# MLP activations transposed by transfers of their 16-bit halves in place of TensorE with the identity

## The chip, the cores and the metric

The kernel runs on one core of a Trainium2 chip. A core has TensorE (matmuls, called PE in the profile), VectorE (DVE), ScalarE (ACT), GpSimd (POOL) and SyncE (SP), each with its own instruction queue, which is worked off in order, and 16 DMA engines that all queues share. The metric is the device time of one execution in microseconds; the median of several runs counts.

## What is computed

One layer of a diffusion backbone for 128 context tokens and 128 latent tokens, all in float32: a modulation from the conditioning vectors, one combined projection, two attention mixers, a gated merge, and an MLP with a squared ReLU. The part that the change touches:

```python
def sq_relu_mlp(h, w_up, w_down):
    return jnp.square(jax.nn.relu(h @ w_up)) @ w_down

        h2 = rms_norm(xp, norm2_w[l]) * (1 + sc2) + sh2
        xp = xp + g2 * sq_relu_mlp(h2, w_up[l], w_down[l])
```

`D_MODEL` is 2048 and the hidden width `D_FF` is 8192. The same weights serve both groups of tokens, so a weight tile that is loaded once is used for two blocks of 128 tokens.

## The kernel before

Every float32 product is made as three products of a reduced float32 type: the weight tile (`raw`, 128 partitions x 1024, 512 KB) is copied by ScalarE into a high part `wH`, VectorE subtracts to get the low part `wL` (`split`, lines 86 and 234), and TensorE multiplies high by high, high by low and low by high (lines 284 to 286). A weight tile is one step; a plain step is twelve matmuls of 128x512.

All weight tiles stand in one list, `wsteps`. For each step `run()` issues the loads that are due, prepares (splits) the tiles ahead, issues the matmuls, and then calls what is hung on that step with `at(...)`. Two tables by step decide how far ahead this goes: `LOOK` (splits) and `RUN` (loads). For some tiles (`LO_DMA`, `XL_DMA`) the low part is made by ScalarE and an adding transfer of GpSimd instead of VectorE. All tiles of 128x1024 come from one pool of 48 buffers, so a load waits until a buffer is free.

The MLP is the last stage. `w_up` has 16 slices of 512 columns, two to a piece; `w_down` has the matching 16 groups of rows. The order is: up products of piece 0, then for p from 0 to 7 the up products of piece p+1 (`up_pair`) followed by the down products of piece p (`down_unit`, four output slices of four steps, 16 steps). In `up_pair` a position of 256 rows is either plain (two steps, 24 matmuls) or fast: a seven-product scheme after Strassen and Winograd, with 21 matmuls, and with more sums on VectorE and copies on ScalarE. `FAST` lists the fast positions of each piece. At the end of a piece VectorE combines the partial products, and ScalarE applies ReLU and square (`up`, line 1176).

The square of the ReLU then lies with tokens on partitions, and the down product needs the hidden units there. `up_T(n)` does this for slice n: `tT` (line 797 and following) makes eight 128x128 transposes on TensorE against the identity into PSUM, ScalarE copies the high part from PSUM into `aH`, VectorE subtracts for `aL`. `T_PAIR` says, for each piece, at which of the 16 down steps of the piece before this is done; slices 0 and 1 have their own places (two steps after the up product, and inside the first fast position of piece 1). The down products of a piece are used one piece later, so these results are not needed at once.

Sums of the down products over the pieces go to `dsum`: by VectorE, or for the units in `SUM_DMA` by a ScalarE copy and an adding transfer of GpSimd. `AWAY` lists gate tiles of the merge that go to memory and come back `GATE_BACK` steps before they are used, to free buffers.

Of the kernel before, what the change touches and what calls it, by code (L numbers as in the profile page):

```python
# [10 lines left out]
F32 = mybir.dt.float32  # L11
F32R = mybir.dt.float32r
BF16 = mybir.dt.bfloat16
AF = mybir.ActivationFunctionType
OP = mybir.AluOpType
AX = mybir.AxisListType

P = 128
# [10 lines left out]
PIECES = [[2 * i, 2 * i + 1] for i in range(8)]  # L29
# [1 line left out]
LOAD = 4  # L31
FB_DVE = 6
FB1 = 14
H_AT = 41
DOTS1 = [6, 8, 15, 20, 28, 30, 31, 38]
CHUNKS = [2, 2, 2, 4, 6]
NFAST = 8
FAST = {1: (0, 1, 5, 6, 7), 2: (0, 3, 4, 6, 7), 3: (0, 2, 4, 5, 7), 4: (0, 2, 3, 5, 7), 5: (0, 1, 2, 4, 5, 7), 6: (0, 2, 4, 6, 7), 7: (0, 1, 2, 4, 5, 7)}
SUM_DMA = [5, 6, 9, 10, 11, 12, 13, 15, 16, 19, 20, 21, 23, 25, 27]
AWAY = [('gA', 1), ('gB', 0), ('gA', 2)]  # L40
GATE_BACK = 3
DIRECT = (3,)
LO_DMA = [70, 83, 86, 107, 131, 176, 184, 186, 196, 233, 242, 292, 314, 328, 357, 379, 402, 435]
LO_AHEAD = 2

LOOK = "523112344222344433223333332123333453344534332454455544344533333544324554444555556665556644444333333333332222122213444544555434333333342344333334333323445565533344456656533344434444445455564546555554444443322355444554433333333434334433333333333654654332334455554444555653323314333422222223443233333332223323365455454443222212233432443334434743443332222333423323333333333325434322223333433323333334555543365365433333332222554442122132334343222223332233345544"
RUN = "454562331000011222223333322222222222222233345555544455434445554445665555555664543433234334444445665543321222222212444444444444442222222232223344444455544544444444443344343334466644455555554543255444343355556866544443566553333323333345552332222222223445332333333333332211122222332233322211233323323332333223333333332343322211333343333322233333444433643333312222334443322333233322222222322333443434455544333120222222232111233456655566567556322325335553333333"
CONST_AT = [60, 65]
XL_DMA = [40]
ADA_AT = [None, 4, 13, 21, 21, 34, 30]  # L50
XS_AT = {1: 13, 2: 18, 3: 29}
POST = {('kvA', 0): [67, 69, 71], ('qA', 0): [70, 73, 75], ('qA', 1): [74, 76, 82], ('kB', 0): [78, 84, 89], ('qB', 0): [82, 84, 93], ('kB', 1): [85, 90, 93], ('qB', 1): [91, 94, 96]}
JOBS = [[78, 79, 81, 83, 94], [82, 83, 87, 90, 94], [88, 89, 91, 93, 98], [93, 93, 95, 98, 102], [96, 97, 100, 105, 112], [102, 103, 107, 112, 120], [105, 107, 111, 118, 120], [112, 114, 117, 120, 122]]
SS_AT = [48, 56, 66, 75, 139, 139]
T_AT = [4, 4]
PREP_IN = [6, 7]
DOTS = [32, 39, 41, 43, 47, 47, 48, 49, 51, 52, 53, 55, 60, 64, 67, 69, 72, 76, 76, 83, 89, 90, 92, 92, 94, 98, 101, 103, 103, 105, 108, 111, 111, 112, 115, 118, 120, 122, 123, 123, 124, 128, 129, 129, 131, 132, 133, 137, 137, 137, 138, 143, 144, 147, 147, 150, 153, 157, 158, 160, 165, 167, 168, 168, 170, 172, 175, 177, 177, 178, 179, 183]
DOTS2 = [232, 233, 235, 237, 240, 242, 262, 265, 269, 270, 272, 289, 297, 299, 302, 306, 307, 326, 327, 332, 334, 335, 358, 361, 364, 365, 368, 370, 393, 394, 397, 401]
STAT_AT = [-1, -1, 10, 12]
# [5 lines left out]
def tile_hybrid_step(ctx: ExitStack, tc: tile.TileContext, a):  # L65
# [10 lines left out]
    def G(name, dt=F32):  # L76
        return gp.tile([P, 1024], dt, name=name, tag="g")
# [7 lines left out]
    def copy(out, in_):  # L85
        act.activation(out, in_, AF.Copy)  # L86
# [99 lines left out]
    wsteps = []  # L186
    cal = {}

    def at(i, fn):
        cal.setdefault(i, []).append(fn)  # L190
# [361 lines left out]
    def end_of(key):  # L552
        return max(st["i"] for st in wsteps if st["key"] == key)
# [238 lines left out]
    def tT(src, hi, lo):  # L792

        for s in range(2):
            ps = bank("ps_T")
            for k in range(4):
                pe.transpose(ps[:, k * P:(k + 1) * P], src[:, s, k * P:(k + 1) * P], ident)  # L797
            psv = ps.rearrange("p (k t) -> p k t", k=4)
            copy(hi[:, :, s, :], psv)
            dve.tensor_tensor(lo[:, :, s, :], psv, hi[:, :, s, :].bitcast(F32), op=OP.subtract)  # L800

    def HL(name):
        return [G(name + x, F32R).rearrange("p (k s t) -> p k s t", k=4, s=2) for x in "HL"]
# [254 lines left out]
    def up_pair(p):  # L1058
# [32 lines left out]
        for pos, is_fast in enumerate(kinds):  # L1091
# [50 lines left out]
            def mm_y(st, b=b, j=j, pos=pos, end=end):  # L1142
                u0, u1 = (G(f"up{n}").rearrange("p (s n) -> p s n", s=2) for n in (n0, n1)) if end else (None, None)
                if end:
                    copy(u0[:, 0, :], box["Q1"])
                lo, hi = slice(0, 512), slice(512, 1024)
                todo = [("Q6", sc(j, 1), b["uH"][:, lo], b["uL"][:, lo]), ("Q2", x(j, 1, 0), b["YB"][:, lo], b["YB"][:, hi]),
                        ("Q7", sc(j, 2), b["tH"][:, hi], b["tL"][:, hi]), ("Q4", x(j, 1, 1), b["uH"][:, hi], b["uL"][:, hi]),
                        ("Q5", sc(j, 0), b["tH"][:, lo], b["tL"][:, lo])]
                if end or pos == 0:  # L1150
                    todo.append(("Q3", sc(j, 3), b["XH"][:, hi], b["XL"][:, hi]))
                if not end:
                    todo = [todo[i] for i in ((1, 2, 0, 4, 5, 3) if pos == 0 else (1, 4, 2, 3, 0))]
# [13 lines left out]
                for name, stat, h, l in todo:  # L1167
                    mm(name, stat, h, l, end)
                    for out, i0, i1, op in post.get(name, []):
                        dve.tensor_tensor(out, *(box[v] if isinstance(v, str) else v for v in (i0, i1)), op=op)  # L1170
                b.clear()
                if end:
                    for n, u in ((n0, u0), (n1, u1)):
                        up_r[n] = u
                        for f in (AF.Relu, AF.Square):
                            act.activation(u.rearrange("p s n -> p (s n)"), u.rearrange("p s n -> p (s n)"), f)  # L1176
                    box.clear()
# [271 lines left out]
```

## Time and profile before

| | us |
|---|---|
| runs | 1347.2, 1346.38, 1343.57 |
| median | 1346.38 |
| the profiled execution | 1346.98 |
| its span, first to last instruction | 1344.9 |

The profile is of one execution. Busy times are given by engine and by stretch of time; a busy TensorE is not TensorE at its peak, because matmuls overlap and each row shows a matmul's whole passage, so its pace is read from the starts of matmuls that follow each other. The MLP's weight steps run from about 675 us to the end; the transposes of line 797 for the MLP lie between 681 and 1288 us, sixteen groups of eight. In this kernel ScalarE issues one transfer of its own, at the start; all weight loads are issued by SP. In a row of the groups stand line, engine, operation, names, shapes and count, then busy us and mean ns, then the idle time before, with what ended it. In a timeline row stand start, length, engine, line, operation, names, count, and in brackets the idle time before it.

### The profile page before, as it was taken

What the parts mean: (1) busy time and instruction counts of PE and PEld (TensorE: products, weight loads), DVE (VectorE), ACT (ScalarE), POOL (GpSimd) and SP (SyncE); (2) the same over time, 40 slices, a digit from 0 to 9 for tenths busy, and PEclk for the clock granted to TensorE, in tenths of its full rate; (3) what the DMA queues carried; (4) which work ended last, traced back from release to release, by engine and by line L of the source; (5) the groups of instructions that cost most, each with busy time, mean ns of one, the idle gap of its engine ahead of it and who ended that gap; (6) DMA issues with size and microseconds to landing.
All of it is one profiled execution on the core that took longest, in us unless ns stands there. A gap on an engine that the chain in (4) does not pass through costs nothing.

```text
span 1344.9 us, 18331 instructions
## 1 busy us (share of the span) xinstructions
PE 1331.6 (99%) x6552; PEld 1081.6 (80%) x6552; DVE 1194.9 (89%) x1568; ACT 738.8 (55%) x966; POOL 66.7 (5%) x76
## 2 busy tenths in 40 slices
PE   8899999999999999999999999999999999999998
PEld 4577788888788878888888888888888888888887
DVE  4689999988898999998789999998999999899675
ACT  5524443566656544345666665565665656556540
POOL 0000001332000000000000000000000000000000
PEclk9899999999999999999999999999999999999999
DMA  9999998977688999798466666888798887769942
GB/s 370 410 409 408 404 366 352 375 215 271 193 282 299 377 397 344 284 332 290 175 232 230 240 219 245 271 264 279 231 317 239 265 285 216 267 191 302 373 151 93
DMA packets 109611, 385.44 MB, mean 287 GB/s; under 512 B 12368, under 2 KB 13584, under 8 KB 109520
## 3 DMA queue, kind: packets, MB, share of 16 engines
q1 hardware_dynamic: 104064, 365.05, 73.5%
q0 software_dynamic: 5312, 19.14, 7.5%
q8 instruction: 51, 0.84, 0.3%
q14 instruction: 40, 0.33, 0.1%
q10 hardware_dynamic: 144, 0.08, 0.0%
HBM read 369.25 MB, written 7.11 MB: 280 GB/s over the span
## 4 chain that ended last, share of the span: by engine, by line
PE 96%; DMA 3%; DVE 1%; issue 0%; ACT 0%; SPq 0%; DVEq 0%
PE acc L284 17%; PE acc L286 17%; PE acc L285 17%; PE Q L1068 6%; PE Q L1070 6%; PE Q L1069 6%; PE acc L384 4%; PE acc L386 4%; PE acc L385 4%; PE ps_ada L301 2%; DMA raw<-in_w_in 2%; PE ps_T L797 1%; PE ps_S L700 1%; DMA araw<-in_w_pair 1%; PE Z L1070 1%; PE Z L1069 1%
## 5 line engine op out<-in xcount | busy, mean ns | idle before, releaser
L234 DVE TENSOR_TENSOR wL<-raw,wH 128x1024 fp32r<-128x1024 f32 x361 | 430.7, 1225 | 79.6 <-ACT wH L86 72.6
L86 ACT ACTIVATE wH<-raw 128x1024 fp32r<-128x1024 f32 (+1 forms) x385 | 385.6, 1047 | 138.6 <-PE acc L285 33.0
L384 PE MATMUL acc<-wH,hH 128*128 128x512 f32 x276 | 109.9, 398 | 0.0
L386 PE MATMUL acc<-wH,hL 128*128 128x512 f32 x276 | 108.4, 393 | 0.7 <-DVE hL L90 0.7
L385 PE MATMUL acc<-wL,hH 128*128 128x512 f32 x276 | 108.5, 393 | 0.0
L284 PE MATMUL acc<-wH,hH 128*128 128x512 f32 x256 | 101.8, 398 | 0.0
L286 PE MATMUL acc<-wH,hL 128*128 128x512 f32 x256 | 99.8, 390 | 0.0
L285 PE MATMUL acc<-wL,hH 128*128 128x512 f32 x256 | 99.7, 389 | 0.0
L1278 DVE CUSTOM_DVE_ANT_0 aT<-aT,cB,cols 128x1024 f32<-128x1024 f32 x56 | 71.5, 1284 | 0.2
L1278 DVE CUSTOM_DVE_ANT_0 junk<-aT,cB,cols 128x1024 bf16<-128x1024 f32 x56 | 71.3, 1279 | 0.0
L86 ACT ACTIVATE tH<-t 128x1024 fp32r<-128x1024 f32 x37 | 39.3, 1062 | 56.9 <-DVE t L1123 42.0
L384 PEld LDWEIGHTS acc<-wH,hH 128*128 128x128 f32 x276 | 52.3, 190 | 14.2 <-issue 3.3
L386 PEld LDWEIGHTS acc<-wH,hL 128*128 128x128 f32 x276 | 52.4, 190 | 12.3 <-DVE hL L90 1.1
L385 PEld LDWEIGHTS acc<-wL,hH 128*128 128x128 f32 x276 | 52.4, 190 | 10.5
L86 ACT ACTIVATE uH<-raw 128x1024 fp32r<-128x1024 f32 x37 | 39.3, 1063 | 36.2 <-DVE raw L1128 35.2
L286 PEld LDWEIGHTS acc<-wH,hL 128*128 128x128 f32 x256 | 48.1, 188 | 10.3
L285 PEld LDWEIGHTS acc<-wL,hH 128*128 128x128 f32 x256 | 48.1, 188 | 9.6 <-issue 0.2
L284 PEld LDWEIGHTS acc<-wH,hH 128*128 128x128 f32 x256 | 48.1, 188 | 9.6 <-issue 0.2
L1123 DVE TENSOR_TENSOR t<-raw 128x1024 f32<-128x1024 f32 x37 | 45.1, 1220 | 5.8 <-PE Z L1069 1.9
L1176 ACT ACTIVATE up<-up 128x1024 f32<-128x1024 f32 x28 | 29.7, 1062 | 33.0 <-DVE up L1170 32.6
L86 ACT ACTIVATE dsum<-acc 128x512 f32<-128x512 f32 x38 | 22.0, 595 | 45.2 <-PE acc L286 42.1
L1133 DVE TENSOR_TENSOR uL<-raw,uH 128x1024 fp32r<-128x1024 f32 x37 | 45.1, 1219 | 0.1
(629 smaller groups left out, 3320.4 us busy)
## 6 DMA issues: line engine op xcount, KB each, us to landing
raw<-in_w_in SPq DMA_DIRECT2D x133, 512.0 KB, 6.7
raw<-in_w_down SPq DMA_DIRECT2D x128, 512.0 KB, 5.9
araw<-in_w_pair SPq DMA_DIRECT2D x80, 512.0 KB, 9.6
raw<-in_w_upF SPq DMA_DIRECT2D x74, 512.0 KB, 5.2
aT<-in_w_gT SPq DMA_DIRECT2D x64, 512.0 KB, 6.6
raw<-in_w_up SPq DMA_DIRECT2D x54, 512.0 KB, 5.1
aT<-in_w_adaT SPq DMA_DIRECT2D x48, 512.0 KB, 7.4
raw<-in_w_out SPq DMA_DIRECT2D x32, 512.0 KB, 9.5
```

The costliest lines, as they stand in the source:

```text
L86: act.activation(out, in_, AF.Copy)
L234: dve.tensor_tensor(st["lo"], st["raw"], st["hi"].bitcast(F32), op=OP.subtract)
L284: pe.matmul(acc[tb], sh, wh[:, k, :], start=f, stop=False)
L285: pe.matmul(acc[tb], sh, wl[:, k, :], start=False, stop=False)
L286: pe.matmul(acc[tb], sl, wh[:, k, :], start=False, stop=l)
L384: pe.matmul(acc[tb], sh, wh[:, k, :], start=kt == 0 and k == 0, stop=False)
L385: pe.matmul(acc[tb], sh, wl[:, k, :], start=False, stop=False)
L386: pe.matmul(acc[tb], sl, wh[:, k, :], start=False, stop=last and k == 1)
L1068: pe.matmul(acc, stat[0], hi, start=f, stop=False)
L1069: pe.matmul(acc, stat[0], lo, start=False, stop=False)
L1070: pe.matmul(acc, stat[1], hi, start=False, stop=l)
L1278: dve.tensor_tensor_reduce(out, box["raw"], cB[s, tag], 1.0, dst if second else baT[:, part, fb:fb + 1], OP.mult, OP.add, dst)
```

## The change

`up_T` no longer uses TensorE. It is cut in two. `up_planes(n)` splits each 32-bit word of the activation into its two 16-bit halves: two ScalarE copies from a strided 16-bit view of the tile into two planes of 128x1024, and after each a transposing transfer of that plane, 256 KB from SBUF to SBUF, issued from ScalarE's queue. Some steps later `up_T(n)` puts the transposed halves together again with four ScalarE copies of 128x512 16-bit values into a float32 tile, and splits that tile as a whole (one copy, one subtraction of 128x1024). `P_PAIR` and `P_UP` place the first part, `T_PAIR` and `T_UP` the second. Per slice two transfers, six 16-bit copies and one 128x1024 split stand in place of eight transposes, two 128x512 copies and two 128x512 subtractions from PSUM.

Most tables are also set anew: fast positions fall from 37 to 35 (pieces 1 and 4 have four), `SUM_DMA` from 15 units to 14, `LO_DMA` from 18 tiles to 17, `XL_DMA` rises from one to two, two more gate tiles go to memory and back, and some digits of `LOOK` and `RUN` and some places in the early stages move by a step or a few.

```diff
-H_AT = 41
+H_AT = 37
-FAST = {1: (0, 1, 5, 6, 7), 2: (0, 3, 4, 6, 7), 3: (0, 2, 4, 5, 7), 4: (0, 2, 3, 5, 7), 5: (0, 1, 2, 4, 5, 7), 6: (0, 2, 4, 6, 7), 7: (0, 1, 2, 4, 5, 7)}
-AWAY = [('gA', 1), ('gB', 0), ('gA', 2)]
-GATE_BACK = 3
+FAST = {1: (0, 1, 5, 7), 2: (0, 2, 3, 6, 7), 3: (0, 2, 4, 5, 7), 4: (0, 2, 5, 7), 5: (0, 1, 2, 3, 5, 7), 6: (0, 2, 4, 6, 7), 7: (0, 1, 2, 4, 6, 7)}
+AWAY = [('gA', 1), ('gB', 0), ('gA', 2), ('gA', 0), ('gB', 2)]
+GATE_BACK = 4
...
-T_PAIR = [[11, 11], [7, 15], [13, 13], [16, 16], [9, 9], [12, 12], [12, 12]]
+T_PAIR = [[5, 9], [8, 12], [8, 10], [9, 11], [8, 11], [10, 11], [8, 11]]
+P_PAIR = [[1, 4], [4, 6], [4, 5], [5, 6], [4, 6], [6, 6], [4, 6]]
+P_UP = [2, 2]
+T_UP = [6, 7]
...
+    def halves(name):
+        return gp.tile([P, 2048], U16, name=name, tag="g")
+
+    planes = {}
+
+    def up_planes(n):
+        src = up_r.pop(n).rearrange("p s n -> p (s n)").bitcast(U16).rearrange("p (c h) -> p h c", h=2)
+        pl, planes[n] = halves(f"pl{n}"), halves(f"plT{n}")
+        for h in range(2):
+            copy(pl[:, 1024 * h:1024 * h + 1024], src[:, h, :])
+            act.dma_start_transpose(planes[n][:, 1024 * h:1024 * h + 1024].rearrange("p (j t) -> p j t", t=P),
+                                    pl[:, 1024 * h:1024 * h + 1024])
+
     def up_T(n):
         aH[n], aL[n] = HL(f"a{n}")
-        tT(up_r.pop(n), aH[n], aL[n])
+        full = G(f"aF{n}")
+        dst = full.bitcast(U16).rearrange("p (k s t h) -> p h s k t", k=4, s=2, h=2)
+        pT = planes.pop(n).rearrange("p (h s k t) -> p h s k t", h=2, s=2, k=4)
+        for h in range(2):
+            for st in range(2):
+                copy(dst[:, h, st], pT[:, h, st])
+        split(aH[n].rearrange("p k s t -> p (k s t)"), aL[n].rearrange("p k s t -> p (k s t)"), full)
...
-        if n != PIECES[0][1]:
-            at(end_of(("up", n)) + 2, lambda: up_T(n))
+        at(end_of(("up", n)) + P_UP[n], lambda: up_planes(n))
+        at(end_of(("up", n)) + T_UP[n], lambda: up_T(n))
...
-                    if p == 1:
-                        up_T(PIECES[0][1])
...
-            for n, i in zip(PIECES[p + 1], T_PAIR[p]):
-                at(len(wsteps) + i, lambda n=n: up_T(n))
+            for n, i, j in zip(PIECES[p + 1], P_PAIR[p], T_PAIR[p]):
+                at(len(wsteps) + i, lambda n=n: up_planes(n))
+                at(len(wsteps) + j, lambda n=n: up_T(n))
```

More of the change, by code (lines that the diff above doesn't have):

```diff
@@ L13 @@
 BF16 = mybir.dt.bfloat16
+U16 = mybir.dt.uint16
 AF = mybir.ActivationFunctionType
@@ L37 @@
 NFAST = 8
-FAST = {1: (0, 1, 5, 6, 7), 2: (0, 3, 4, 6, 7), 3: (0, 2, 4, 5, 7), 4: (0, 2, 3, 5, 7), 5: (0, 1, 2, 4, 5, 7), 6: (0, 2, 4, 6, 7), 7: (0, 1, 2, 4, 5, 7)}
-SUM_DMA = [5, 6, 9, 10, 11, 12, 13, 15, 16, 19, 20, 21, 23, 25, 27]
-AWAY = [('gA', 1), ('gB', 0), ('gA', 2)]
-GATE_BACK = 3
+FAST = {1: (0, 1, 5, 7), 2: (0, 2, 3, 6, 7), 3: (0, 2, 4, 5, 7), 4: (0, 2, 5, 7), 5: (0, 1, 2, 3, 5, 7), 6: (0, 2, 4, 6, 7), 7: (0, 1, 2, 4, 6, 7)}
+SUM_DMA = [5, 6, 9, 10, 11, 12, 15, 19, 20, 21, 23, 25, 26, 27]
@@ L42 @@
+AWAY = [('gA', 1), ('gB', 0), ('gA', 2), ('gA', 0), ('gB', 2)]
+GATE_BACK = 4
 DIRECT = (3,)
-LO_DMA = [70, 83, 86, 107, 131, 176, 184, 186, 196, 233, 242, 292, 314, 328, 357, 379, 402, 435]
+LO_DMA = [70, 83, 86, 107, 131, 176, 184, 196, 233, 242, 292, 314, 328, 357, 379, 402, 435]
 LO_AHEAD = 2
-LOOK = "523112344222344433223333332123333453344534332454455544344533333544324554444555556665556644444333333333332222122213444544555434333333342344333334333323445565533344456656533344434444445455564546555554444443322355444554433333333434334433333333333654654332334455554444555653323314333422222223443233333332223323365455454443222212233432443334434743443332222333423323333333333325434322223333433323333334555543365365433333332222554442122132334343222223332233345544"
@@ L50 @@
[L50 to L54, printed above, removed]
-T_AT = [4, 4]
@@ L59 @@
-STAT_AT = [-1, -1, 10, 12]
-T_PAIR = [[11, 11], [7, 15], [13, 13], [16, 16], [9, 9], [12, 12], [12, 12]]
+LOOK = "423112345333444433223333332123333453344534332454455544344533333544324554444555556665556644444333333333332222122213444544555434333333342344333334333323445565533345456656533344434444445455564547666654444443322355444554433333333434334433333333333654654332334455443444555653323314332311122223443233333332223323365455454443222212233432443334434743443332222333423323333333333325434322223333433323333334555543365365433233332222554442122132334343222223332233345544"
@@ new lines @@
+RUN = "454562220000011222223333322222222222222233345555555455434445554445665555555664543433234334444445665543321222222212444444444444442222222232223344444455544544444444443344333334466644455555554543255444343355556866555554566553333323333345552332222233334556443443333333332211122222332233322211233323323332333223333333332343322211333343333322233333444433643332212222334443322333233322222222322333443434455544333120222222232111233456655566567556322325335553333333"
+CONST_AT = [59, 65]
+XL_DMA = [40, 45]
@@ new lines @@
+ADA_AT = [None, 4, 13, 21, 21, 35, 30]
+XS_AT = {1: 11, 2: 18, 3: 30}
+POST = {('kvA', 0): [67, 69, 71], ('qA', 0): [70, 73, 75], ('qA', 1): [74, 76, 82], ('kB', 0): [79, 83, 88], ('qB', 0): [82, 84, 92], ('kB', 1): [84, 89, 92], ('qB', 1): [91, 94, 96]}
+JOBS = [[78, 79, 81, 83, 94], [82, 83, 87, 90, 94], [88, 89, 91, 93, 98], [93, 93, 95, 98, 102], [96, 97, 100, 105, 112], [102, 103, 107, 112, 120], [105, 107, 111, 118, 120], [112, 114, 118, 121, 123]]
+SS_AT = [49, 56, 66, 75, 139, 139]
+T_AT = [4, 4]
@@ new lines @@
+PREP_IN = [4, 7]
+DOTS = [32, 39, 40, 42, 47, 47, 48, 49, 51, 52, 53, 55, 60, 64, 67, 69, 72, 76, 76, 83, 89, 90, 92, 93, 94, 98, 101, 103, 103, 105, 108, 111, 111, 112, 115, 118, 120, 122, 123, 123, 124, 128, 129, 129, 131, 132, 133, 137, 137, 137, 138, 143, 144, 147, 147, 150, 153, 157, 158, 159, 164, 166, 167, 167, 169, 171, 176, 176, 177, 178, 182, 187]
+DOTS2 = [232, 233, 235, 237, 240, 242, 262, 265, 269, 270, 272, 289, 297, 299, 302, 306, 307, 326, 327, 332, 334, 335, 358, 361, 364, 365, 368, 370, 393, 395, 397, 401]
@@ L61 @@
+STAT_AT = [-1, -2, 10, 11]
+T_PAIR = [[5, 9], [8, 12], [8, 10], [9, 11], [8, 11], [10, 11], [8, 11]]
+P_PAIR = [[1, 4], [4, 6], [4, 5], [5, 6], [4, 6], [6, 6], [4, 6]]
+P_UP = [2, 2]
+T_UP = [6, 7]
 COL = {"qA": 0, "kvA": 1024, "qB": 1536, "kB": 2560, "vB": 3584, "gA": 4608, "gB": 6656}
```

6 lines of the change are left out of this document (removed).

## The prediction

> **What bounds the kernel now.** I read the page first, then the sums by stretch, then single rows of the MLP stage.
>
> ```profile
> span 1344.9 us, 18331 instructions
> PE 1331.6 (99%) x6552; PEld 1081.6 (80%) x6552; DVE 1194.9 (89%) x1568; ACT 738.8 (55%) x966; POOL 66.7 (5%) x76
> PE 96%; DMA 3%; DVE 1%; issue 0%; ACT 0%; SPq 0%; DVEq 0%
> ```
>
> The chain that ended last is 96% TensorE. A busy TensorE need not be at its peak, so the stretches come next (busy time and count for each engine, granted clock, DMA share and rate).
>
> ```profile
> core 0: us, PE busy (x) PEld busy (x) DVE busy (x) ACT busy (x) POOL busy (x), PEclk, DMA share, GB/s
> 0.00:60.00 60.00, 51.47 (x308) 29.14 (x308) 28.73 (x53) 33.40 (x56) 2.00 (x10) 0.94 1.00 388
> 500.00:675.00 175.00, 175.00 (x806) 145.64 (x805) 158.24 (x222) 90.71 (x123) 5.05 (x8) 1.00 0.81 288
> 675.00:1345.00 670.00, 665.17 (x3000) 551.76 (x2998) 601.80 (x700) 393.09 (x449) 21.63 (x25) 1.00 0.74 245
> ```
>
> The MLP stage is the last 670 us. VectorE is busy for 90% of it, ScalarE for 59%, the DMA engines for 74%. Whether TensorE waits there is read from starts: first the 1st and the 9th weight step of the down products of piece 0, eight steps of twelve matmuls apart; then the transposes of two slices between two matmuls.
>
> ```profile
> 739.67 0.39 PE L284 MATMUL acc<-wH,a0H 128*128 128x512 f32 x1
> ...
> 761.43 0.39 PE L284 MATMUL acc<-wH,a0H 128*128 128x512 f32 x1
> ...
> 1286.34 0.39 PE L286 MATMUL acc<-wH,a12L 128*128 128x512 f32 x1
> 1286.57 1.91 PE L797 MATMUL ps_T<-ident,up 128*128 128x128 f32 x16
> 1288.24 0.48 PE L284 MATMUL acc<-wH,a12H 128*128 128x512 f32 x1
> 1288.55 0.40 PE L285 MATMUL acc<-wL,a12H 128*128 128x512 f32 x1
> ```
>
> (761.43 - 739.67) / 96 = 0.227 us from matmul to matmul, 2.72 us a step. 3000 instructions in 670 us, of which 128 are transposes, are (670 - 5 of tail - 128 x 0.11) / 2872 = 0.227 us each: TensorE runs at this pace through the whole stage, with no gap. So only TensorE work that goes away shortens it, and any new lateness of a weight tile lengthens it.
>
> **The change part by part.** *Removed from TensorE:* all transposes of MLP activations.
>
> ```profile
> L797 PE MATMUL ps_T<-ident,up x128: 270/272/273, 681.4 to 1288.2; 128*128 128x128 f32 x128
> ```
>
> A row says 272 ns, but they overlap. From L286 at 1286.34 to L285 at 1288.55 are 2.21 us; two matmul paces are 0.45, so sixteen transposes cost 1.76, 0.110 each: 128 x 0.110 = 14.0 us, all on the path. *Added to TensorE:* FAST lists 35 positions instead of 37 (one fewer in pieces 1 and 4). A fast position is 21 matmuls, two plain steps are 24: 6 x 0.227 = 1.4 us. Net -12.7 us.
>
> *ScalarE* gets the work. Rows of its groups in the MLP stretch (busy us, mean ns | idle before):
>
> ```profile
> L86 ACT ACTIVATE wH<-raw 128x1024 fp32r<-128x1024 f32 x172 | 172.2, 1052 | 38.1 <-PE acc L285 8.5 <-DMA raw<-in_w_down 8.5 <-PE acc L286 5.6
> L86 ACT ACTIVATE uH<-raw 128x1024 fp32r<-128x1024 f32 x37 | 39.3, 1063 | 36.2 <-DVE raw L1128 35.2 <-PE acc L285 1.0
> L86 ACT ACTIVATE YB<-raw 128x512 fp32r<-128x512 f32 x37 | 23.0, 621 | 10.1 <-DMA raw<-in_w_upF 5.0 <-PE Q L1069 2.1 <-issue 1.5
> L86 ACT ACTIVATE dsum<-acc 128x512 f32<-128x512 f32 x38 | 22.0, 595 | 45.2 <-PE acc L286 42.1 <-PE acc L285 2.1
> L86 ACT ACTIVATE a3H<-ps_T 128x512 fp32r<-128x512 f32 x2 | 1.1, 628 | 0.0
> ```
>
> Per slice, two plane copies of 128x1024 (by the uH row 1.06 each; the 16-bit form is not in the trace), four copies of 128x512 that put the halves together (0.55 to 0.62 by the a3H and YB rows), and one split of 1.06 come in place of two copies at 0.55: 2.1 + 2.4 + 1.06 - 1.1 = 4.4, times 16 is 71 us. Two fast positions fewer take back 2 x (3 x 1.06 + 0.62) - 4 x 1.05 = 3.4, two sums fewer by POOL 1.2. 393 + 66 = 459 of 657 us, 70%: no bound on the mean, but it comes in bursts, and ScalarE's wH copies feed every matmul.
>
> *The transfers.* 32 are added, 256 KB each, issued from ScalarE's own queue: while it issues one, the next wH waits behind it. The trace has no transposing transfer. Nearest rows: the one transfer that ScalarE issues, a common load on SP, and how those land.
>
> ```profile
> L94 ACTq DMA_DIRECT2D cols<-in_cols x1: 407/407/407, 0.7 to 0.7; - x1
> L208 SPq DMA_DIRECT2D raw<-in_w_upF x74: 327/328/1722, 651.5 to 1226.0; - x74
> DMA to landing us min/median/max: 3.3/6.1/14.7
> ```
>
> Lower bound 0.33 us; upper bound eight such issues, 2.6 us, if each 128x128 square of the 128x1024 source is pushed by itself. I take the ScalarE row, 0.41, the same engine and the same kind of request. Call it X. In piece 1 all four transfers stand one behind the other, so this is where to try it:
>
> ```profile
> 825.07 0.39 PE L284 MATMUL acc<-wH,a2H 128*128 128x512 f32 x1
> ...
> 830.56 2.15 ACT L1176 ACTIVATE up<-up 128x1024 f32<-128x1024 f32 x2 [0.36 <-DVE up L1170]
> 832.62 5.79 ACT L86 ACTIVATE wH<-raw 128x1024 fp32r<-128x1024 f32 x6
> 846.39 1.28 ACT L86 ACTIVATE dsum<-acc 128x512 f32<-128x512 f32 x2 [7.98 <-PE acc L286]
> ```
>
> Down step 0 starts at 825.07 (my zero). The six wH end at 838.41, at 13.3 (0.95 apart: 2.15 for two dependent squares is 1.09 apart, so waiting for an own result costs about 0.1). Then four times (1.06 + 0.1 + X) = 4.6 + 4X; the two evacuations 1.28, possible once TensorE has done step 7 at 21.8; wH of step 10, 0.95; its split on VectorE with the handover, 1.3. Step 10 is due at 27.2. 13.3 + 4.6 + 1.3 + 0.95 + 1.3 + 4X = 21.5 + 4X: in time up to X = 1.4, and beyond that 4 us of stall per us. Today the cover is the idle 7.98 us in the last row. The same sum for the other pieces (they begin 5.4 to 6.8 us after their step 0) has its limit at X = 1.1 (piece 2), 1.5 (3), 2.0 (4), 1.9 (5), 1.45 (6).
>
> Piece 0 is the tight one, its planes come at steps 1 and 4. Its squares end 6.75 us after step 0 (746.42 against 739.67). Up to the wH of step 8 ScalarE has five wH (4.75), four planes with their issues (4.64 + 4X), two evacuations (1.28), one wL copy (1.06), the wH of step 8 itself (0.95): 19.4 + 4X, with the split 20.7 + 4X. At 0.41 that is 22.4 against 21.8, 0.6 late; then the joining and split of slice 2 (2.3 + 1.06) and wH of step 9 make another 1.6. I book 2.2 us for piece 0 and nothing for the rest; at X = 2.6 the same sums give 10.9, 4.7, 6.0, 4.3, 2.3, 2.9 and 4.6, together 35.7. The first two slices, transposed within the up products of piece 1, I book at nothing: the wH there run ahead behind the same kind of idle time.
>
> The joining copies wait for the landing, and with them every later wH and, behind a split that waits for ScalarE, VectorE's queue. In piece 1 the first joining comes about 9 us after its issue, against 6.1 us median landing today.
>
> [...]
>
> *DMA engines, SP, POOL.*
>
> ```profile
> q1 hardware_dynamic: 104064, 365.05, 73.5%
> q0 software_dynamic: 5312, 19.14, 7.5%
> SPq L208 <- PE Q L1070: 137.6, 60, 7.8
> SPq L208 <- PE acc L286: 131.8, 37, 9.3
> ```
>
> q1 uses 0.735 x 1345 / 365 = 2.7 us of all engines per MB, q0 5.3. 32 x 0.26 = 8.4 MB more are 23 to 44 us, in 26% x 670 = 174 us of free time: nothing on the path. A weight load now may have to wait until a transposing transfer that took the same completion counter eight transfers earlier has landed; SP mostly waits for TensorE to free a buffer (the last two rows, its longest waits in the MLP stretch), which covers it. Two more gates that go to memory and back (2.1 MB, 6 us at q1's price) fall where the DMA share is 0.81 and TensorE has no gap: nothing. POOL adds one sum less and one other load more: nothing.
>
> *VectorE.*
>
> ```profile
> L234 DVE TENSOR_TENSOR wL<-raw,wH 128x1024 fp32r<-128x1024 f32 x164 | 194.3, 1220 | 36.7 <-ACT wH L86 34.0 <-issue 2.6
> L1126 DVE TENSOR_TENSOR raw<-t,raw 128x512 f32<-128x512 f32 x37 | 25.6, 692 | 1.3
> 683.65 1.28 DVE L800 TENSOR_TENSOR a0L<-ps_T,a0H 128x512 fp32r<-128x512 f32 x2
> ```
>
> One split of 1.22 per slice for two of 0.64: -1 us. A fast position is four subtractions or sums of 1.22 and three of 0.69, 6.95, against 2.44 for two plain splits: two fewer are -9. Two more sums into dsum: +1.4. About 593 of 657 us: its share stays at 90%, no gain and no loss.
>
> *Start.* Tables of the first stages move by a few steps. TensorE is idle for 8.5 of the first 60 us while the DMA share is 1.00; I allow 2 us either way and take 0.
>
> Sum: profiled execution 1346.98 us (span 1344.9 and 2.1 around it) - 14.0 + 1.4 + 2.2 = 1336.5. The median of the runs, 1346.38, lies 0.6 below that execution, so 1336.
>
> The PSUM banks of the transposes come free, which nothing on the path waits for today; the transposes of slice 1, which stood inside the first fast position, leave it.
>
> **The rivals.** *1, slower: the issue blocks ScalarE.* If X is near 2.6, wH of the steps 8 to 12 come late in each piece: 1346.98 - 12.7 + 35.7 = 1370. It decides from X = 1.7, where the same sums give 12.5 us and the gain is gone. For it: SP's longest issue took 1.72 us, and a destination of 128x8x128 is cut finer than any transfer here. Against it: 512 KB loads cost 0.33 whatever their destination tile.
>
> *2, slower: the transfers land late.* If each takes its queue for 9.6 us, as the longest wait of this kind now, the second half of a slice lands 19 us after the first issue, the joining waits some 10 us, of which 3 are covered: 7 x 16 = 112 us, 1446.
>
> ```profile
> SPq L208 <- DMA dsum<-dsum: 22.8, 4, 9.6
> ```
>
> It decides from a landing of about 12 us. For it: the engines are 74% busy with loads queued ahead. Against it: the median of 6.1 us for twice the bytes. [...]
>
> *3, no change:* X between 1.5 and 1.85, or the start's tables and a late VectorE eating 9 to 13 us: 1342 to 1350.
>
> *4, it does not save what is removed:* if transposes hid in gaps, nothing would come back. The pace of 0.227 on both sides of them excludes all but a trace of it; it is counted in 3.
>
> **How the numbers follow.** Forecast 0.48, rival 1 0.33, rival 2 0.10, rival 3 0.09. 0.3% (4 us) is about what a measurement of this kernel can tell from no change. Faster 0.48, same 0.09, slower 0.43. The forecast's own range is 1332 (TensorE work alone, 1333.7, less 2 for the start) to 1341 (X = 1.4). For 8 in 10 the top must reach into rival 1: 1368 leaves out its last part and rival 2.
>
> **What would show it.** TensorE should show only the 32 transposes of the merge under the helper's line, and still 0.227 us from matmul to matmul between 500 us and the end. The issue on ScalarE's queue shows X: at 0.4 the forecast holds, above 1.7 rival 1. A wait of VectorE's wL for ScalarE's wH well over 34 us, or gaps of TensorE before down steps 8 to 12, show ScalarE late; a wait of the joining copies on the transfers shows rival 2. ScalarE's busy time should be near 805 us, VectorE's near 1186. Wrong prices of the 16-bit copies (over 1.4 us) would move the limits of X below 1 and make it wrong too.

## The result, and the profile after

The changed kernel takes 1409.97 us (median of 4 runs, 1407.19 to 1418.45) against 1346.22 for the kernel before beside it: a ratio of 1.0487, 95% interval 1.044 to 1.0535. Forecast were 1336 and a range of 1332 to 1368. The profiled execution is 1410.92, its span 1409.1. Up to 675 us the two traces agree within a microsecond or two; all of the loss lies in the MLP stage.

From the page of the changed kernel: the span, the busy times, the chain that ended last by engine, and the group of VectorE's splits.

```profile
span 1409.1 us, 18206 instructions
...
PE 1343.6 (95%) x6429; PEld 1079.3 (77%) x6430; DVE 1187.3 (84%) x1544; ACT 804.5 (57%) x1040; POOL 65.1 (5%) x75
...
PE 72%; DMA 7%; ACT 7%; DVE 6%; ACTq 4%; issue 3%; DVEq 0%; SPq 0%
...
L238 DVE TENSOR_TENSOR wL<-raw,wH 128x1024 fp32r<-128x1024 f32 x366 | 436.9, 1225 | 134.3 <-ACT wH L90 133.2
```

The chain was 96% TensorE and is 72% now; ACT and ACTq (ScalarE's own issuing) have entered it, DMA's share has risen from 3% to 7% and VectorE's from 1% to 6%. The busy times of ScalarE (804.5) and VectorE (1187.3) are those forecast (805, 1186): the work was counted rightly, and what was wrong is when it is done. Now the MLP stretch, in the columns used before.

```profile
675.00:1410.00 735.00, 678.49 (x2883) 550.45 (x2881) 594.41 (x675) 460.65 (x525) 21.57 (x25) 0.96 0.78 236
```

2883 instructions in 735 us; before, 3000 stood in 670 without a gap. At the old pace the work left is 665 - 14.0 + 1.4 = 652.4, plus 5 of tail; the stage lasts 734, so 77 us were lost. Taking from each start-to-start distance the usual pace of its kind accounts for 75 of them: about 59 us of gaps, and about 16 us by which TensorE's matmuls were slower at half clock. Both are seen at the worst place, the down products of piece 6. First ScalarE's queue there (a timeline: start, length, what, idle before), then TensorE's.

```profile
1310.64 7.10 ACTq L1004 DMA_TRANSPOSE plT<-pl  x1
1317.79 2.95 ACT L90 ACTIVATE wH<-raw 128x1024 fp32r<-128x1024 f32 x3 [8.64 <-issue]
...
1326.60 11.87 ACTq L1004 DMA_TRANSPOSE plT<-pl  x1
1338.57 1.08 ACT L90 ACTIVATE dsum<-acc 128x512 f32<-128x512 f32 x2 [12.00 <-issue]
1339.54 1.06 ACT L90 ACTIVATE wH<-raw 128x1024 fp32r<-128x1024 f32 x1
```

```profile
1329.34 0.39 PE L290 MATMUL acc<-wH,a12L 128*128 128x512 f32 x1
1340.65 0.80 PE L288 MATMUL acc<-wH,a13H 128*128 128x512 f32 x1 [10.92 <-ACT wH L90]
1341.91 0.80 PE L289 MATMUL acc<-wL,a13H 128*128 128x512 f32 x1 [0.47 <-DVE wL L238]
1342.50 0.63 PE L290 MATMUL acc<-wH,a13L 128*128 128x512 f32 x1
1342.93 0.63 PE L288 MATMUL acc<-wH,a13H 128*128 128x512 f32 x1
```

ScalarE reaches a transposing transfer at 1326.60 and is let go at 1338.5. Two evacuations and the next `wH` have stood behind it in the queue; the `wH` ends at 1340.6, and in that moment TensorE, idle for 10.92 us, goes on. Before some issues ScalarE's queue stands too: in the trace the issues of 1306.80 and 1310.64 follow an idle 0.74 and 1.49 us, and each comes 0.08 us after the landing (1306.72 and 1310.56) of the transfer that last used the same one (103 and 108) of the eight completion counters, 100, 101, 103 to 105 and 108 to 110 in the trace, which SP's loads and ScalarE's transfers take in turn (in the trace of before all 725 transfers of the two queues do). Then its matmuls are 0.43 apart (1342.50 to 1342.93), not 0.227: the granted clock is halved, as a window inside it shows (PEclk is the third number from the end):

```profile
1341.50:1344.00 2.50, 2.09 (x5) 1.71 (x6) 0.35 (x1) 2.47 (x4) 0.00 (x0) 0.50 1.21 174
```

The half clock appears in nine stretches of the stage ahead of its tail, 3.4 to 13.7 us long, 55 us together, each beginning in or behind a gap; before the change there was none. Every stretch is one to four times 3.41 us long. The length of a wait alone does not tell whether one follows: at 760 us two waits of 0.91 and 0.76 us, one matmul apart, were followed by a slow stretch, and one wait of 2.68 us that began at 1235.9 was not.

The transfers themselves, by their line, and ScalarE's two new kinds of copies:

```profile
L1004 ACTq DMA_TRANSPOSE plT<-pl x32: 1248/1255/11867, 683.7 to 1326.6; - x32
...
DMA to landing us min/median/max: 3.1/5.7/20.0
```

```profile
L90 ACT ACTIVATE aF<-plT 128x512 uint16<-128x512 uint16 x64 | 42.4, 766 | 0.0
...
L90 ACT ACTIVATE pl<-up 128x1024 uint16<-128x1024 uint16 x32 | 33.7, 1052 | 33.9 <-issue 28.1 <-PE acc L290 5.8
```

X, the issue time, is 1.25 us at the least and at the median, three times the 0.41 taken, and 11.87 at the worst. Over all 32 rows it adds up to 64.4 us, 24 of them beyond 1.25 each. What waits for it, in the sums of waits in the MLP stage (us, times, longest), of ScalarE, VectorE, TensorE and SP:

```profile
ACT wH L90 <- issue: 30.9, 10, 8.6
...
ACT pl L90 <- issue: 28.1, 17, 2.8
ACT dsum L90 <- issue: 13.7, 2, 12.0
```

```profile
DVE wL L238 <- ACT wH L90: 91.2, 27, 16.6
```

```profile
PE acc L288 <- ACT wH L90: 19.0, 7, 10.9
PE Q L1094 <- ACT dsum L90: 9.4, 3, 6.2
```

```profile
SPq L212 <- DMA plT<-pl: 35.0, 8, 10.4
```

ScalarE's copies wait behind issues, VectorE's splits wait for ScalarE (34.0 us before, 91.2 now), and TensorE for both; `dsum` is an evacuation of the PSUM banks that the next up product (`Q`) needs. The last row is something else: eight weight loads on SP were held until a transposing transfer had landed. The longest of these waits ends at 1325.55, 0.08 us after the transfer of 1306.80, which had used the load's completion counter (103), landed.

At the same place the load rate falls. Three windows, the last number being GB/s:

```profile
1298.00:1306.00 8.00, 8.00 (x37) 6.60 (x37) 4.40 (x6) 7.57 (x8) 0.00 (x0) 1.00 1.03 373
1306.00:1326.00 20.00, 17.37 (x70) 13.74 (x69) 6.09 (x6) 7.51 (x9) 0.86 (x1) 0.91 1.15 233
1326.00:1345.00 19.00, 7.61 (x25) 5.52 (x24) 2.00 (x2) 6.97 (x10) 0.85 (x1) 0.69 1.16 207
```

The DMA engines are full in all three (their share, the number before it, is 1.03 to 1.16), but move 373 GB/s before the first transposing transfer of this piece and 207 to 233 beside them.

So four things can hold the loss: the hold of ScalarE's queue (theory A), a wait of the joining copies for landings (B), transfers that slow or hold the weight loads (C), and the added copies with the new tables. The experiments take them apart.

### The profile page after: what moved, and what is told of

Read it like the earlier page. It is cut to its first block, busy times and chain, and to the rows that moved or that the text cites. A ratio compares the mean times of both kernels' runs of the same rounds, so it can differ in the third digit from the quotient of the medians.

```text
span 1409.1 us, 18206 instructions
## 1 busy us (share of the span) xinstructions
PE 1343.6 (95%) x6429; PEld 1079.3 (77%) x6430; DVE 1187.3 (84%) x1544; ACT 804.5 (57%) x1040; POOL 65.1 (5%) x75
## 4 chain that ended last, share of the span: by engine, by line
PE 72%; DMA 7%; ACT 7%; DVE 6%; ACTq 4%; issue 3%; DVEq 0%; SPq 0%
PE acc L289 11%; PE acc L290 11%; PE acc L288 11%; PE Q L1094 5%; PE Q L1095 5%; PE Q L1096 5%; PE acc L388 4%; PE acc L390 4%; PE acc L389 4%; ACTq L1004 4%; PE ps_ada L305 2%; DMA raw<-in_w_in 2%; DVE wL L238 2%; ACT wH L90 2%; ACT pl L90 2%
## 5 line engine op out<-in xcount | busy, mean ns | idle before, releaser
L238 DVE TENSOR_TENSOR wL<-raw,wH 128x1024 fp32r<-128x1024 f32 x366 | 436.9, 1225 | 134.3 <-ACT wH L90 133.2
L90 ACT ACTIVATE pl<-up 128x1024 uint16<-128x1024 uint16 x32 | 33.7, 1052 | 33.9 <-issue 28.1
L1094 PE MATMUL Q<-tH,sH 128*128 128x512 f32 x70 | 29.6, 423 | 15.5 <-ACT dsum L90 9.4
```

The lines of the kernel that those rows point to most:

```text
L238: dve.tensor_tensor(st["lo"], st["raw"], st["hi"].bitcast(F32), op=OP.subtract)
L1094: pe.matmul(acc, stat[0], hi, start=f, stop=False)
```

## The experiments

All times are medians, the ratio with its 95% interval is to the kernel before on the same chip (1345 to 1346 us in every set). "Hold" is the time that ScalarE's queue is held for the issues, added over their rows, or by what stands in their place, from its start to the start of the next copy. For issues a hand-over comes on top: around the 64 us of rows of the changed kernel ScalarE idles for 72 us.

| kernel | us | ratio | hold on ScalarE, us |
|---|---|---|---|
| before without MLP transposes | 1338.69 | 0.9933 to 0.9971 | none |
| before with the new tables | 1357.35 | 1.0067 to 1.0112 | none |
| changed, no transfers | 1351.33 | 1.0025 to 1.0061 | none |
| changed, plain transfers | 1358.25 | 1.0074 to 1.0119 | 15 |
| changed, transfers from SP | 1358.73 | 1.0081 to 1.0121 | none |
| changed, short fillers | 1363.28 | 1.0115 to 1.0155 | 36 |
| changed, long fillers | 1398.41 | 1.038 to 1.0423 | 72 |
| changed, fewer loads ahead | 1406.95 | 1.0404 to 1.0521 | 60 |
| changed, transfers unread | 1409.44 | 1.0448 to 1.0492 | 66 |
| **changed** | 1409.97 | 1.044 to 1.0535 | 64 |
| changed, old tables | 1415.09 | 1.0493 to 1.0555 | 71 |
| changed, whole transfers | 1417.90 | 1.0466 to 1.0563 | 83 |
| changed, halved transfers | 1430.52 | 1.0606 to 1.0691 | 89 |

**What the removed transposes were worth.** The kernel before, without the eight transposes of a slice: the split reads the square of the ReLU as it lies.

```diff
-        tT(up_r.pop(n), aH[n], aL[n])
+        src = up_r.pop(n)
+        for s in range(2):
+            v = src[:, s, :].rearrange("p (k t) -> p k t", k=4)
+            copy(aH[n][:, :, s, :], v)
+            dve.tensor_tensor(aL[n][:, :, s, :], v, aH[n][:, :, s, :].bitcast(F32), op=OP.subtract)
```

> The kernel of before without the 128 transposes of the MLP: each slice is split where it lies (same copies and subtractions, read from SBUF in place of PSUM); the transposition itself is left out. If TensorE's work is what sets the MLP stage, 128 x 0.110 = 14 us go: 1332 us. If another engine would set it as soon as TensorE has less to do, 1340 to 1346.

1338.7: 7.3 us come back, half of the 14.0. TensorE has gaps it did not have; its largest waits in the MLP are

```profile
PE Q L1072 <- ACT dsum L86: 1.9, 2, 1.1
PE Q L1073 <- DVE XL L1135: 1.1, 2, 0.7
```

so with TensorE quicker the others begin to be late, in many small gaps. No version of this change can be expected below 1338.7, as long as the rest stays.

**The tables.** The new tables with TensorE's transposes, and the changed kernel with the tables of before (only the four tables that place the new parts stay):

```diff
 (before)
-T_PAIR = [[11, 11], [7, 15], [13, 13], [16, 16], [9, 9], [12, 12], [12, 12]]
+T_PAIR = [[5, 9], [8, 12], [8, 10], [9, 11], [8, 11], [10, 11], [8, 11]]
...
 (changed)
-FAST = {1: (0, 1, 5, 7), 2: (0, 2, 3, 6, 7), 3: (0, 2, 4, 5, 7), 4: (0, 2, 5, 7), 5: (0, 1, 2, 3, 5, 7), 6: (0, 2, 4, 6, 7), 7: (0, 1, 2, 4, 6, 7)}
+FAST = {1: (0, 1, 5, 6, 7), 2: (0, 3, 4, 6, 7), 3: (0, 2, 4, 5, 7), 4: (0, 2, 3, 5, 7), 5: (0, 1, 2, 4, 5, 7), 6: (0, 2, 4, 6, 7), 7: (0, 1, 2, 4, 5, 7)}
...
```

> All new tables of the change, with the transposes still on TensorE (at the new steps of T_PAIR; slice 1 where it was). If the tables alone are harmless: 1346.4 + 1.4 for two fast positions fewer = 1348 us, at most 1352. If the loss comes from the tables (fewer loads ahead, gates away, other steps): 1380 to 1410.

> The changed kernel with every table of before that has a counterpart (FAST, AWAY, GATE_BACK, LOOK, RUN, the start's tables); only P_PAIR, T_PAIR, P_UP and T_UP stay new. If the new tables hold a part of the loss (with TensorE's transposes they cost 11 us): 1395 to 1402. If they only follow the transfers: 1410 to 1425.

1357.35 and 1415.09. Beside TensorE's transposes the new tables cost 11 us, more than the 1348 to 1352 of harmless tables and far from the 1380 to 1410 that would make them the loss. Beside the transfers they may gain 5, which the scatter of the two kernels (1413 to 1419 and 1407 to 1418) leaves open; most of the loss is not in them. Which of the tables costs the 11 us was not tried.

**The copies alone, and plain transfers.** The changed kernel without its transfers (the joining copies read the planes as they are), and with plain transfers of the same bytes at the same places.

```diff
-            act.dma_start_transpose(planes[n][:, 1024 * h:1024 * h + 1024].rearrange("p (j t) -> p j t", t=P),
-                                    pl[:, 1024 * h:1024 * h + 1024])
+            act.dma_start(planes[n][:, 1024 * h:1024 * h + 1024], pl[:, 1024 * h:1024 * h + 1024])
```

> The changed kernel without its 32 transposing transfers: all ScalarE copies stay, and the joining copies read the planes directly; the transposition is left out. If the loss comes from issuing or landing the transfers: 1334 to 1342 us. If ScalarE's 112 added copies are enough to make it late: 1385 to 1410.

> The changed kernel with plain transfers of the same 256 KB from plane to plane in place of the transposing ones; the transposition is left out. If the long issue of a transposing transfer (1.25 us and more, against 0.33 to 0.41 for a plain one) or its own slowness in the DMA engines makes the loss: 1334 to 1345 us. If any 256 KB transfer between SBUF tiles, queued among the weight loads, lands too late: 1370 to 1410.

1351.3 and 1358.3, both between the ranges expected. Even transfers that cost nothing would leave this kernel 5 us behind the one before: against 1338.7 the copies and tables cost 12.6. How this divides between copies and tables is not shown; the tables alone cost 11 beside TensorE's transposes. In the kernel without transfers TensorE waits longest for an evacuation that stands behind ScalarE's other work:

```profile
PE Q L1092 <- ACT dsum L90: 7.3, 3, 4.4
```

The plain transfers tell that their number and bytes are worth 7 us. They issue in 0.47 us, close to the 0.41 of the forecast, and land in 5.0 us at the median against 5.7, though in 8.7 and not 20.0 at worst; being transposing costs another 52 us.

```profile
L1004 ACTq DMA_DIRECT2D plT<-pl x32: 472/472/520, 682.5 to 1284.6; - x32
...
DMA to landing us min/median/max: 2.3/5.0/8.7
```

In the DMA engines the two are not alike either. The rows of ScalarE's queue (packets, MB, share of the time of 16 engines), of the changed kernel and of this one:

```profile
q10 hardware_dynamic: 33936, 8.48, 4.4%
```

```profile
q10 hardware_dynamic: 4752, 8.47, 1.7%
```

For the same bytes that is 0.044 x 1409 = 62 us of all engines against 0.017 x 1357 = 23.

**Who pays: the reader, the queue, or the loads.** Two edits of the changed kernel. In the first the transfers are issued as ever, but the joining copies read the planes that ScalarE wrote; in the second SP issues them.

```diff
 (unread)
-        pl, planes[n] = halves(f"pl{n}"), halves(f"plT{n}")
+        pl, plT = halves(f"pl{n}"), halves(f"plT{n}")
+        planes[n] = pl
...
 (from SP)
-            act.dma_start_transpose(planes[n][:, 1024 * h:1024 * h + 1024].rearrange("p (j t) -> p j t", t=P),
+            sync.dma_start_transpose(planes[n][:, 1024 * h:1024 * h + 1024].rearrange("p (j t) -> p j t", t=P),
```

> The changed kernel, but the joining copies read the planes as ScalarE wrote them and not what the transfers wrote: the 32 transposing transfers are issued at the same places and go through the same buffers, but no joining copy waits for a landing (the transposition is left out). Theory A (the issue holds ScalarE's queue, 40 us of regular issue plus the blocked ones): about as slow as the changed kernel, 1395 to 1415. Theory B (the joining copies wait for late landings): near the kernel with plain transfers, 1355 to 1365. Theory C (the transposing packets slow the weight loads beside them, whoever issues or reads them): 1395 to 1415 like A; the next two runs tell A from C.

> The changed kernel with the 32 transposing transfers issued from SP's queue and not from ScalarE's; all else stays. Theory A (the issue holds ScalarE): ScalarE loses the hold, 1355 to 1370. Theory C (the transposing packets slow the weight loads): 1395 to 1415, or more, since SP's load issues now stand behind the blocked ones.

1409.4 and 1358.7. The joining copies' waiting for a landing costs nothing (theory B falls; SP's loads still wait 35.6 us for landings in that kernel); taking the issue off ScalarE brings back 51 us. SP's rows of that kernel:

```profile
L1004 SPq DMA_TRANSPOSE plT<-pl x32: 1237/1288/7397, 683.7 to 1282.7; - x32
...
DMA to landing us min/median/max: 3.1/4.3/18.0
```

The issue takes SP as long as it took ScalarE (1.29 us at the median against 1.25), blocked ones of up to 7.40 us too, 62 us in all; but SP mostly waits anyway (543 of the stage's 682 us, by the rows of its waits), and the kernel ends with plain transfers' time. Issue times and landings (3.1 to 18.0 us, and 3.1 to 20.0 from ScalarE) are much the same from either queue; the loss comes with the queue that the issues stand in.

**The hold rebuilt without transfers.** In place of each transfer, ScalarE copies 16-bit values for about as long, into the buffer that the transfer would fill: once the same short copy at each place, once by a list of the 32 recorded issue times.

```diff
-            act.dma_start_transpose(planes[n][:, 1024 * h:1024 * h + 1024].rearrange("p (j t) -> p j t", t=P),
-                                    pl[:, 1024 * h:1024 * h + 1024])
+            copy(fill[:, 0:1216], flat[:, 0:1216])
...
+    hold = [1.33, 1.25, 1.25, 1.25, 1.25, 3.75, 1.25, 1.25, 1.25, 2.28, 1.25, 1.63, 1.26, 1.61, 1.48, 2.42,
+            2.01, 1.25, 1.25, 1.46, 1.25, 1.25, 1.25, 1.26, 1.31, 1.91, 1.25, 1.25, 1.25, 7.10, 1.71, 11.87]
...
+            left = hold.pop(0) + 0.17
+            parts = -(-int(left * 1000) // 1800)
+            w = int((left / parts - 0.1) / 0.000833)
+            for _ in range(parts):
+                copy(fill[:, 0:w], flat[:, 0:w])
```

> The changed kernel with each transposing transfer replaced by a ScalarE copy of about the same hold (128x1216 of 16 bits, 1.25 us by the median issue) into the buffer that the transfer would fill; no transfer is left, the joining copies read the planes as they are (the transposition is left out). Theory A in its regular part (32 x 1.25 us of ScalarE): 1375 to 1390, against 1351 without transfers. If only the blocked issues, the landings or the loads beside them matter: 1352 to 1362.

> The changed kernel without transfers, with ScalarE held at each of the 32 places by copies for as long as the issue there took in the trace of the changed kernel (1.25 us at most places, 3.75, 7.10 and 11.87 at the worst; 64 us in all, and the 0.17 us of hand-over around each). No DMA packet is added; the joining copies read the planes as they are (the transposition is left out). Theory A in full (the hold of ScalarE's queue, regular and blocked, is the whole loss): 1395 to 1412. Theory D (half of it: the rest are weight loads that run beside the transposing packets or wait on SP until a transfer has landed): 1375 to 1390.

The short fillers gave 1363.3. From a filler's start to that of the next copy are 1.11 us (two rows of its timeline), 35.5 us for 32:

```profile
749.17 1.20 ACT L90 ACTIVATE plT<-up 128x1216 uint16<-128x1216 uint16 x1
750.28 1.04 ACT L90 ACTIVATE pl<-up 128x1024 uint16<-128x1024 uint16 x1
```

That is 12 us more than without transfers, far below the expected 1375 to 1390 and near the range for no effect of regular holds (1352 to 1362): short holds are covered for two thirds. The forecast's own sums give about 5 us at X = 1.1, all in piece 0. The long fillers gave 1398.4, within the 1395 to 1412 expected if the hold is the whole loss, with no transfer in the kernel and the same kind of wait. From their starts to the next copies are 72.0 us, as much as ScalarE idles around the issues of the changed kernel.

```profile
PE acc L288 <- ACT wH L90: 17.2, 6, 13.1
```

So 36 us more of hold (72.0 - 35.5), 24 of them in place of the issues that took over 1.25 us, cost 35 us: what stands in a lump is not covered, and the half clock is part of the price (about 12 us here, by the same reckoning as the 16 above). The hold explains 47 of the 59 us between 1351.3 and 1410.0. The other 12 are what moving transposed data adds while ScalarE is held: loads that are slower, or that SP holds until a transfer has landed (35.0 us of such waits). Which of these two it is was not taken apart. When SP issues, no more than 7 us of it are left (1358.7 against 1351.3), and SP's own row there is

```profile
SPq L212 <- DMA plT<-pl: 5.3, 1, 5.3
```

This speaks for the held loads, and does not show it, since ScalarE is not held there.

**What sets X, and the block.** The same bytes cut in two (64 transfers of four 128x128 squares) and in one (16 of sixteen squares), and fewer weight loads ahead around the blocked issues of piece 6.

```diff
 (halved)
+            for q in (1024 * h, 1024 * h + 512):
+                act.dma_start_transpose(planes[n][:, q:q + 512].rearrange("p (j t) -> p j t", t=P), pl[:, q:q + 512])
...
 (whole)
+        act.dma_start_transpose(planes[n].rearrange("p (j t) -> p j t", t=P), pl)
...
 (fewer ahead)
-            while loads and loads[0][0] <= st["i"] + int(RUN[st["i"]]):
+            ahead = min(int(RUN[st["i"]]), 3 if st["i"] in few else 9)
+            while loads and loads[0][0] <= st["i"] + ahead:
...
+        if p == last - 1:
+            few.update(range(len(wsteps) - 8, len(wsteps) + 10))
```

> The changed kernel with each transposing transfer cut in two of four 128x128 squares (64 issues on ScalarE's queue). If the issue costs by squares: 0.63 us median each, the same 1.25 us per half slice, and 1400 to 1415. If it costs by instruction: 1.25 us each, 40 us more on ScalarE, and 1430 to 1460.

> The changed kernel with one transposing transfer of 128x2048 for each slice in place of two of 128x1024: 16 issues on ScalarE's queue, the same bytes. If an issue costs by instruction: 1.25 us each, 20 us less hold, the last pair's block stays, 1380 to 1398. If it costs by bytes above some size: 2.5 us each, the same hold, 1402 to 1415.

> The changed kernel with weight loads at most 3 steps ahead, not 5 or 6, from 8 steps before the down products of piece 6 to 10 steps into them; all else stays. If the blocked issues there (7.10 and 11.87 us) come from loads queued beside the transfers, they fall under 3 us, TensorE's 11 us gap at 1329 us goes, and the time is 1390 to 1400. If the transposing transfers block one another, whatever is loaded: both stay and the time is 1405 to 1415.

The issue rows of the halved, the whole, and the kernel with fewer loads ahead (ns, min/median/max):

```profile
L1005 ACTq DMA_TRANSPOSE plT<-pl x64: 1206/1286/5237, 681.9 to 1351.3; - x64
```

```profile
L1004 ACTq DMA_TRANSPOSE plT<-pl x16: 1737/4045/10720, 684.2 to 1336.2; - x16
```

```profile
L1007 ACTq DMA_TRANSPOSE plT<-pl x32: 1247/1278/7895, 680.9 to 1320.9; - x32
```

The shortest issue is 1.21 us for four squares, 1.25 for eight, 1.74 for sixteen: a nearly fixed price up to eight. What goes beyond the shortest is 12 us in all for halves, 24 for the changed kernel, 55 for whole slices: in these three the block grows with the bytes of a transfer. So a halved issue costs by instruction, as one branch of its expectation had it, and a whole one costs neither 1.25 nor 2.5, so that both branches of the other missed. The three times, 1410, 1418 and 1431, stand in the order of the holds, 64, 83 and 89 us.

With fewer loads ahead the two worst issues of piece 6 fell from 7.10 and 11.87 to 3.53 and 7.89, and TensorE's gap there from 10.92 to 5.65; I had expected issues under 3. In the kernel with transfers unread, whose loads run as in the changed one, the two took 7.98 and 13.02. So queued loads are a part of the block, not all of it, as far as one trace of each can tell. The total moved within its scatter (1401.57 to 1413.93). What blocks an issue stays open; an issue did not wait until the transfer before it had landed, since the one of 1310.64 was let go at 1317.7 and its forerunner landed at 1325.5.

**Looking for a better version.** From SP, three more: the joining copies on GpSimd; whole transfers; whole transfers with the tables of before.

```diff
 (GpSimd)
-                copy(dst[:, h, st], pT[:, h, st])
+                pool.tensor_copy(dst[:, h, st], pT[:, h, st])
```

> The kernel that issues the transfers from SP (1358.7), with the 64 joining copies on GpSimd and not on ScalarE, queued there right behind the transfers. ScalarE loses 49 us of work. If ScalarE's added work is what keeps that kernel behind the one of before: 1340 to 1350. If SP's load issues that stand behind the transfers, or the tables, keep it behind: 1354 to 1362. If GpSimd's copies are slow (over 2 us each) the splits come late: 1365 or more.

> The same whole transfers issued from SP's queue. If SP's own issue time holds that kernel back (1358.7 with 32 of them): 1350 to 1356. If it is ScalarE's copies with the new tables: 1356 to 1361, no change.

> Whole transfers from SP's queue with the tables of before (FAST, AWAY, GATE_BACK, LOOK, RUN, the start's tables). The new tables cost 11 us beside TensorE's transposes and gained 5 beside the transfers on ScalarE's queue. If they are worth less than the old ones once ScalarE isn't held: 1343 to 1352. If they pay here too: 1360 to 1370.

1374.92 (ratio 1.0177 to 1.0241), 1361.39 (1.0077 to 1.0134) and 1368.18 (1.014 to 1.018). GpSimd needs 1.73 us, by a profile that is rough on this engine, for a joining copy that takes ScalarE 0.77:

```profile
L1012 POOL COPY aF<-plT x64: 764/1730/1780, 685.4 to 1307.0; 128x512 uint16<-128x512 uint16 x64
```

Halving the number of SP's issues gained nothing (they took 51 us in all, against 62), and the old tables lost 7 us against the new ones, as the branch "if they pay here too" had it. No version beat the kernel before.

## Why the prediction was wrong, point by point

The forecast was a chain of terms on 1347. What each was, from the medians above:

| step | forecast | measured | from |
|---|---|---|---|
| transposes leave TensorE | -14.0 | -7.3 | 1346.0 to 1338.7 |
| copies on ScalarE, two fast positions fewer, tables | +1.4 | +12.6 | 1338.7 to 1351.3 |
| hold of ScalarE's queue by the issues | +2.2 | +47 | 1351.3 to 1398.4 |
| transposing traffic beside the loads | 0 | +12 | 1398.4 to 1410.0 |

**The step that failed is X.** "I take the ScalarE row, 0.41, the same engine and the same kind of request": the plain transfers bear that price out (0.47), but a transposing one issues in 1.25, and now and then in 7 to 12. The second half of that was not in the sum at all. Every limit (X = 1.1 in piece 2 to 2.0 in piece 4) was worked out for an even X. At 1.25 the same sums give 6 us, and even holds of about that size, the short fillers, cost 12: the limits were right in kind and a few us too wide. One issue of 11.87 in piece 6 passes any limit by itself. The 2.2 stood for copies and issues of piece 0 alone, and that place was not the worst: its four issues took 7.5 us, for which the sum gives 8, and the trace shows waits of 0.91, 0.76 and 0.94 us there; the first two slices, booked at nothing, came with a gap of 4.39 us at 700.

**The removal** was right in mechanism, since the pace of 0.227 held wherever TensorE neither waited nor ran at half clock, and mis-sized: a stage with no gap has no slack on TensorE, but that does not mean that the others have 14 us of it. The 32 transposes of the merge are the only ones left, as forecast.

**ScalarE's 66 us of copies** were counted rightly (joining copies 0.77, not 0.55 to 0.62, but overlapped, 0.66 apart). "No bound on the mean, but it comes in bursts" was the right worry, and outside piece 0 no price was put on it. The forecast looked at `wH`; besides it (19.0 us of TensorE's waits) the evacuation of the banks for the next up product was late (9.4).

**The tables** were booked at +1.4 for the two fast positions and at nothing for the rest; by themselves they cost 11 us beside TensorE's transposes.

**The transfers in the DMA engines and on SP**, "nothing on the path", failed by 12 us. The waits of loads for a landed transfer, which the prediction named and took as covered, are 35.0 us in SP's row. The bytes were counted rightly (8.4 MB more), and their price was too low: 62 us of all engines, where 23 to 44 were reckoned.

**The half clock** was nowhere in the sum; it adds about 16 us, a fifth of the 77 us lost, to gaps made by other things.

**The rivals.** Rival 1 (the issue blocks ScalarE) is what happened. Its condition, X near 2.6 and deciding from 1.7, fits the mean of 64.4 / 32 = 2.0 and not the median; its price, 1370, was too low because it spread X evenly and had no half clock. Rival 2 (late landings make the joining copies wait) fell: with the copies not waiting at all, 1409.4. The landings took 5.7 us at the median and 3.1 at best, where it decided from about 12. The upper bound behind rival 1's 2.6, an issue for each of eight squares, does not hold here: four squares took 1.21 us, eight 1.25 and sixteen 1.74 at the least. Rival 3 (no change) is excluded by the interval, rival 4 by the 7.3 us that did come back. The marks that the prediction set, X on ScalarE's queue and VectorE's wait for `wH` well over 34 us, were the ones that told.

## What to carry to other kernels

A request put on a compute engine's queue costs what that queue has waiting behind it: price it by its worst case at its place, not by a median of another kind of request, and put it on a queue that has nothing urgent, where some 62 us of issuing cost 7 and not 59. When the bounding engine shows no gap, removing its work pays only up to the slack of the next ones (here 7.3 of 14.0 us); a run with that work simply left out tells the ceiling first. A gap on TensorE of a few microseconds can cost more than itself, since the half clock behind it has to be added (here 16 us to 59).

## What was not expected of the hardware

- A transposing transfer inside SBUF holds the queue that issues it for 1.21 us (four squares of 128x128, 16 bit), 1.25 (eight) or 1.74 (sixteen) at the least, and eight squares for up to 11.87 (13.02 in the kernel with transfers unread, 7.89 with fewer loads ahead); a plain one of 256 KB for 0.47. SP is held as ScalarE is, for 1.24 to 7.40.
- Beside transposing transfers the full DMA engines (shares of 1.15 and 1.16) moved 207 to 233 GB/s, against 373 just before (1.03). 32 transposing transfers took 62 us of all 16 engines, the same bytes in plain ones 23.
- The landing of a transposing transfer of 256 KB took 3.1 us at best and 20.0 at worst, with loads queued beside it; a plain one 2.3 to 8.7.
- In and after gaps of TensorE the granted clock was 0.50 for 3.4 to 13.7 us, once after two waits of 0.91 and 0.76 us only.
- GpSimd's copy of 128x512 16-bit values between strided views takes 1.73 us, ScalarE's 0.77.
